# Overflow tables at the end of the expert stage, and the first two experts' transposes behind other products

## The chip, the cores and the metric

The program runs on one core of a Trainium2 chip. The metric is the device time of one execution in microseconds (us). The kernel before was run three times.

## The reference, cut to what matters

One encoder layer over 1024 tokens of width 1024: a combined projection, differential attention and an S5 state-space mixer side by side, an output projection with a first LayerNorm, and a hierarchical mixture of experts (4 groups of 8, two experts for each token) with a second LayerNorm. The change lies in the mixture of experts:

```python
def block_fn(args):                       # one block of 128 rows of one expert
    tok, w, e = args
    xb = h2d[tok]
    hid = jax.nn.silu(xb @ w_gate[e]) * (xb @ w_up[e])
    yb = hid @ w_down[e]
    return yb * w[:, None].astype(yb.dtype)
...
out = jnp.zeros_like(h2d).at[row_tok].add(ys.reshape(n_rows, -1).astype(h2d.dtype))
...
x = _layernorm(alpha * h + moe, ln2_g[i], ln2_b[i])
```

There are 32 experts. Each has a gate and an up matrix of 1024x512 and a down matrix of 512x1024, all in float32 (6 MB for each expert).

## The kernel before, in words

The early stages (projections, state-space mixer, attention, output projection, router) end at about 555 us of the profiled execution. The expert stage then runs to about 1152 us, and a closing stage adds up the two results of each token, normalizes and stores.

**One expert** takes up to 128 tokens. GpSimd gathers their rows (`gather`, L1136) into a slot of `gx`. `tokens(e)` (L1196) transposes the rows on TensorE, eight 128x128 transposes into the PSUM tile `xT`, and `split` (L172) turns that into a high part (a cast on ScalarE) and a low part (a subtraction on VectorE) in `xe`; a product of float32 numbers is made from three products of such parts. `product(e, m)` runs the matrix products, 12 for each half matrix: (e, g0), (e, u0), (e, g1), (e, u1), and later (e, d0), (e, d1). `gate` (silu on ScalarE) and `gated` (a product on VectorE) make the hidden rows, `turn_hidden` transposes them (four transposes into `hT`) and splits them into `he`, and `result` scales and adds on ScalarE and VectorE, scatters the rows to `moe_dram` (L1141) and gathers the rows of expert e+5.

**The weights** come in 192 half matrices of 1 MB, in the order of the list `order`: the gate and up halves of expert e, then the down halves of expert e-1. SyncE loads each (`load_next`) into a ring of 12 slots (15 at the start), so half matrix n is loaded once number n-12 has been split. `split_next` splits each into a ring of three pairs of slots: behind product n stands the split of half matrix n+3, and it waits until product n has read its pair. The loop at L1344 writes these steps in one order, and `keep_order` pins that order on all five engines from the first gather on. An instruction therefore waits behind everything that stands before it on its engine.

**The overflow tables.** An expert with more than 128 tokens needs further blocks. `overflow_blocks` (L1256) counts the tokens of each expert (one product `counts` on TensorE, L1265), makes `meta` (how many further blocks, and of which expert), and then `place` and `blk` (which token stands where), in 25 small VectorE instructions over a borrowed ring slot, the area `over`. Before the change `load_next` calls it where half matrix 63 is loaded, in the middle of the expert stage, about at expert 7.

**After the last expert** SyncE loads the second LayerNorm's gain and offset into the tile `lnc` (L1368 and L1369, 512 KB each, one row copied to all partitions). Each engine reads the number of further blocks from `meta` (L1375), and a loop over them follows (L1376). With these inputs it runs no turn, but its entry and exit are a meeting point: SyncE waits there until every engine has arrived and every transfer has landed. Behind it SyncE loads the rows of `moe_dram` into `mo` (L1444, L1446), GpSimd adds others on the way (L1452), VectorE takes the moments, and the normalized rows go out.

The PSUM banks of the gate and up products are two in all (`bank`, L131): g and u of expert 1 take over the banks of g and u of expert 0, and so wait until `gate(0)` and `gated(0)` have read them.

Of the kernel before, what the change touches and what calls it, by code (L numbers as in the profile page):

```python
# [19 lines left out]
P = 128  # L20
# [3 lines left out]
KT = D // P  # L24
NH = 4
NG = 32
NE = 32
# [87 lines left out]
def tile_kernel(ctx: ExitStack, tc: tile.TileContext, I: dict, out: bass.AP, dbg=None):  # L115
# [9 lines left out]
    sl = Slots()  # L125
# [982 lines left out]

    w_g, w_u, w_d = I["w_exp_gate"][0], I["w_exp_up"][0], I["w_exp_down"][0]
    NRAW, NSPL, NXG = 12, 3, 5  # L1110
    NOVER = 63

    NLENT = 3
    raw_ring = early + sl.take(NRAW + NLENT - len(early))
# [29 lines left out]
    order = []  # L1144
# [14 lines left out]

    def load_next():  # L1160
        n = st_["load"]
        if n == NOVER:
            over.extend(overflow_blocks(deep(n)[0]))
        e, m = order[n]
        j = int(m[1])
        slot = deep(n)[0]
        if m[0] == "d":
            r = sl.at(slot, [P, 2, D], F32, f"rw{e}{m}")
            src = w_d[e, 256 * j:256 * j + 256, :].rearrange("(p k) n -> p k n", p=P)
            for ks in (slice(0, 1), slice(1, 2)) if n == len(order) - 1 else (slice(0, 2),):  # L1170
                SP.dma_start(r[:, ks, :], src[:, ks, :])
        else:
            r = sl.at(slot, [P, 4, 512], F32, f"rw{e}{m}")
            src = w_g if m[0] == "g" else w_u
            SP.dma_start(r, src[e, 512 * j:512 * j + 512, :].rearrange("(p k) n -> p k n", p=P))
        raws[e, m] = r
        st_["load"] += 1
# [15 lines left out]
        hls[e, m] = (a, b)  # L1193
        st_["split"] += 1

    def tokens(e):  # L1196

        g_ = gx(e)
        b_ = bank2(f"xT{e}")
        for kt in range(KT):  # L1200
            PE.transpose(b_[:, kt * P:(kt + 1) * P], rows(g_, kt), ident)  # L1201
        xT[e] = t_ = xes[e % 2]
        split(t_[:, 0], t_[:, 1], b_.rearrange("p (k q) -> p k q", k=KT))

    def gate(e):
        S.activation(hd[:, 0, :], acc.pop((e, "g")), AF.Silu)
# [44 lines left out]
            gather(gx(e + NXG), idx[:, 0, e + NXG:e + NXG + 1])  # L1251


    over = []

    def overflow_blocks(key):  # L1256
        op = Area(sl, 1, "over", key)

        def rtile(name, shape):
            return op.get(f"{name}{shape}", shape)  # L1260

        m128 = rtile("m128", [7])
        ts(m128, iof[:, 1:8], float(P), ALU.mult)
        pr = bank("counts", 1)[:, 0:NE]
        PE.matmul(pr, one, Sx[:, NT, :], start=True, stop=True)  # L1265
        ovc = rtile("wide", [NE, 7])
        V.tensor_tensor(out=ovc, in0=bc(pr, 2, [NE, 7]), in1=bc(m128, 1, [NE, 7]), op=ALU.is_gt)
        ovn = rtile("ovn", [NE])
        V.tensor_reduce(out=ovn, in_=ovc, axis=AX.X, op=ALU.add)
        onef = rtile("onef", [NE])  # L1270
        V.memset(onef, 1.0)
        ove = rtile("ove", [NE])
        V.tensor_tensor_scan(out=ove, data0=onef, data1=ovn, initial=0.0, op0=ALU.mult, op1=ALU.add)
        ovs = rtile("ovs", [NE])
        sub(ovs, ove, ovn)
        metaf = rtile("metaf", [1 + MAXOV])
        V.tensor_copy(metaf[:, 0:1], ove[:, NE - 1:NE])
        for j in range(0, MAXOV, 5):
            ocmp = rtile("wide", [5, NE])
            V.tensor_tensor(out=ocmp, in0=bc(ove, 1, [5, NE]), in1=bc(iof[:, j:j + 5], 2, [5, NE]), op=ALU.is_le)  # L1280
            V.tensor_reduce(out=metaf[:, 1 + j:6 + j], in_=ocmp, axis=AX.X, op=ALU.add)
        ts(metaf[:, 1:1 + MAXOV], metaf[:, 1:1 + MAXOV], float(NE - 1), ALU.min)
        meta = cp.tile([P, 1 + MAXOV], I32, name="meta")
        V.tensor_copy(meta, metaf)
        ob = rtile("ob", [2, NT])
        for k in range(2):
            to = rtile("wide", [NT, NE])
            mul(to, bc(ovs, 1, [NT, NE]), O[:, k])
            V.tensor_reduce(out=ob[:, k], in_=to, axis=AX.X, op=ALU.add)
        q7 = rtile("q7", [2 * NT, 7])  # L1290
        V.tensor_tensor(out=q7, in0=bc(rk.rearrange("p k t -> p (k t)"), 2, [2 * NT, 7]),
                        in1=bc(m128, 1, [2 * NT, 7]), op=ALU.is_ge)
        qd_ = rtile("qd_", [2, NT])
        V.tensor_reduce(out=qd_.rearrange("p k t -> p (k t)"), in_=q7, axis=AX.X, op=ALU.add)
        place = cp.tile([P, 2, NT], F32, name="place")
        stt(place, qd_, -float(P), rk, ALU.mult, ALU.add)

        blk = cp.tile([P, 2, NT], F32, name="blk")
        add(blk, ob, qd_)
        stt(blk, qd_, 1.0, blk, ALU.min, ALU.mult)  # L1300
        ts(blk, blk, 1.0, ALU.subtract)
        op.close()
        return meta, place, blk

    def keep_order():

# [32 lines left out]
    with tc.issue_after(routed.ins), tc.issue_after(turned.ins):  # L1339
        split_next()  # L1340
        split_next()
        tokens(0)
        split_next()
    for n, (e, m) in enumerate(order):  # L1344
        refill()
# [6 lines left out]
            gated(e)  # L1352
        if m == "d1":
            result(e)
        if m == "u1" and e == 0:
            turn_hidden(0)
        if st_["split"] < len(order):
            split_next()
        if m == "u1" and e + 1 < NE:
            tokens(e + 1)  # L1360
        if m == "d0" and e + 1 < NE:
            turn_hidden(e + 1)
    keep_order()
    meta, place, blk = over
    sl.back([deep(n)[0] for n in range(len(order) - NRAW, len(order))])

    lnc = sl.get([P, 2, D], F32, "lnc")
# [148 lines left out]
```

## Time and profile before

| what | value |
|---|---|
| median of 3 runs | 1210.49 us (1209.18 to 1210.93) |
| the profiled execution | 1210.23 us, its span 1208.3 us |
| TensorE busy, share of the span | 1085.0 us, 90% |
| VectorE busy | 971.7 us, 80% |
| ScalarE busy | 704.4 us, 58% |
| GpSimd busy | 357.2 us, 30% |
| read from and written to HBM | 254.12 MB and 27.26 MB |
| granted TensorE clock, mean | 0.939 of full speed |

Engine names in rows: PE is TensorE's matrix products, PEld its weight loads, DVE is VectorE, ACT is ScalarE, POOL is GpSimd, SP is SyncE; a name with q is that engine's queue of instructions. Times are microseconds from the start of the span. `out<-in` gives what an instruction writes and reads, and brackets give how long its engine had been idle before it and what ended that.

### The profile page before, as it was taken

How to read it: one execution, taken by the hardware profiler on the slowest of the kernel's cores; microseconds unless marked ns; L12 is line 12 of the kernel's file. 1: busy time of each engine (PE TensorE's matmuls, PEld its weight loads, DVE VectorE, ACT ScalarE, POOL GpSimd, SP SyncE). 2: the span in 40 equal slices, each digit the busy share in tenths (PEclk: the TensorE clock that was granted, in tenths of full speed). 3: DMA queues.
4: the chain of work that ended last, by engine and by line, in shares of the span. 5: the costliest groups of instructions: out<-in, count | busy, mean ns of one | idle time of the engine just before them, and what ended most of it. 6: DMA issues, size and time to landing. Idle time of an engine off the chain costs nothing. (4 is left out here: it accounts for less than half of the span.)

```text
span 1208.3 us, 15031 instructions
## 1 busy us (share of the span) xinstructions
PE 1085.0 (90%) x5313; PEld 902.5 (75%) x5313; DVE 971.7 (80%) x1409; ACT 704.4 (58%) x941; POOL 357.2 (30%) x279
## 2 busy tenths in 40 slices
PE   7997998898899999995899998999999999999900
PEld 5876787776688788884688877888888888888800
DVE  4598578557877674456799999999999999999848
ACT  3222333445675643223588886888888888888702
POOL 0058455322344452342022121221122122121024
PEclk9998999998899999986899998999999999999955
DMA  5641111211101464454599998999999999999075
GB/s 198 157 89 48 43 40 45 58 36 36 55 16 36 140 214 140 191 207 175 196 358 387 375 369 313 374 385 392 379 379 380 379 375 386 393 377 389 29 258 175
DMA packets 89213, 271.01 MB, mean 224 GB/s; under 512 B 30128, under 2 KB 50608, under 8 KB 64688
## 3 DMA queue, kind: packets, MB, share of 16 engines
q1 hardware_dynamic: 65968, 245.18, 54.0%
q0 software_dynamic: 11216, 23.61, 6.8%
q10 hardware_dynamic: 11952, 1.23, 0.8%
q8 instruction: 43, 0.70, 0.2%
q14 instruction: 34, 0.28, 0.1%
HBM read 254.12 MB, written 27.26 MB: 233 GB/s over the span
## 5 line engine op out<-in xcount | busy, mean ns | idle before, releaser
L1141 POOL DMA_INDIRECT moe_dram<-yo,idx x32 | 54.0, 1688 | 461.9 <-DVE yo L164 456.6
L233 PE MATMUL proj<-xh,wb 128*128 128x512 f32 x256 | 76.2, 410 | 1.6 <-ACT ssm L674 1.6
L233 PE MATMUL proj<-xh,wa 128*128 128x512 f32 x256 | 76.0, 403 | 1.6 <-ACT ssm L674 1.6
L1071 PE MATMUL mix<-woh,mx 128*128 128x512 f32 x256 | 73.8, 399 | 0.7 <-DVE mx L155 0.7
L1136 POOL DMA_INDIRECT gx<-h_dram,idx x32 | 60.3, 1884 | 24.0 <-DVE WT L161 14.6
L786 ACT ACTIVATE p<-s,nm 128x1024 f32<-128x1024 f32 (+7 forms) x64 | 47.2, 742 | 25.3 <-DVE nm L799 19.6
L233 PEld LDWEIGHTS proj<-xh,wb 128*128 128x128 f32 x256 | 50.1, 199 | 12.2 <-ACT ssm L674 1.8
L233 PEld LDWEIGHTS proj<-xh,wa 128*128 128x128 f32 x256 | 48.5, 193 | 11.3 <-ACT ssm L674 1.8
L1071 PEld LDWEIGHTS mix<-woh,mx 128*128 128x128 f32 x256 | 47.6, 190 | 10.3 <-DVE mx L155 1.2
L1247 ACT ACTIVATE yo<-y,WT 128x1024 f32<-128x1024 f32 (+1 forms) x33 | 36.0, 1093 | 31.3 <-PE y L1231 31.3
L781 PE MATMUL s<-kk,qh 128*128 128x512 f32 (+3 forms) x96 | 41.1, 428 | 11.2 <-ACT p L786 10.3
L164 DVE SCALAR_TENSOR_TENSOR yo<-gx,first,yo 128x1024 f32<-128x1024 f32 (+1 forms) x33 | 41.2, 1252 | 6.3 <-ACT yo L1247 5.6
L799 DVE TENSOR_REDUCE nm<-s 128x1 f32<-128x1024 f32 (+3 forms) x32 | 32.6, 1020 | 13.1 <-PE s L783 13.1
L233 PE MATMUL proj<-xl,wa 128*128 128x512 f32 x128 | 42.8, 404 | 0.0
L233 PE MATMUL proj<-xl,wb 128*128 128x512 f32 x128 | 42.6, 408 | 0.0
L1201 PEld LDWEIGHTS xT<-ident,gx 128*128 128x128 f32 x256 | 36.5, 207 | 8.1 <-DMA gx<-h_dram,idx 6.0
L1201 PE MATMUL xT<-ident,gx 128*128 128x128 f32 x256 | 37.1, 290 | 5.7 <-DMA gx<-h_dram,idx 5.7
L155 DVE TENSOR_TENSOR xe<-xT,xe 128x1024 fp32r<-128x1024 f32 x32 | 39.0, 1218 | 3.9 <-ACT xe L174 3.9
L1071 PE MATMUL mix<-wol,mx 128*128 128x512 f32 x128 | 42.0, 397 | 0.0
L819 PE MATMUL po<-vv,half 128*128 128x128 f32 x288 | 41.3, 283 | 0.2 <-ACT half L816 0.2
L174 ACT CAST xe<-xT 128x1024 fp32r<-128x1024 f32 x32 | 32.1, 1004 | 12.6 <-PE xT L1201 12.6
L174 ACT CAST wb<-misc 128x512 fp32r<-128x512 f32 x16 | 9.7, 622 | 47.9 <-DMA misc<-in_w_in_dram 38.3
(862 smaller groups left out, 3560.8 us busy)
## 6 DMA issues: line engine op xcount, KB each, us to landing
misc<-in_w_in_dram SPq DMA_DIRECT2D x16, 512.0 KB, 4.1
mo<-moe_dram SPq DMA_DIRECT2D x11, 512.0 KB, 8.7
xr<-in_x_dram SPq DMA_DIRECT2D x8, 512.0 KB, 6.5
wo_raw<-in_w_out_dram SPq DMA_DIRECT2D x4, 1024.0 KB, 4.8
xa<-in_x_dram SPq DMA_DIRECT2D x8, 512.0 KB, 4.7
h_dram<-xa SPq DMA_DIRECT2D x8, 512.0 KB, 4.8
out_dram<-mo SPq DMA_DIRECT2D x8, 512.0 KB, 3.0
mo<-moe_dram POOLq DMA_DIRECT2D x5, 512.0 KB, 12.3
```

What stands on the lines that cost most here:

```text
L155: eng.tensor_tensor(out=out_, in0=a, in1=b, op=ALU.subtract)
L164: return V.scalar_tensor_tensor(out=out_, in0=a, scalar=s, in1=b, op0=op0, op1=op1)
L174: S.copy(hi, raw)
L233: PE.matmul(o[:, hs], wt[kt // 4][:, w_, kt % 4, :], x_[:, hs], start=(kt == 0 and n == 0), stop=(kt == KT - 1 and n == 2))
L781: PE.matmul(s_[:, c0:c0 + w], qd[0][:, c, tk], kk[h][:, c, c0:c0 + w], start=True, stop=False)
L786: S.activation(p_[:, c, 0:n], s_[:, 0:n], AF.Exp, bias=nm[:, c:c + 1], accum_out=L[:, j, c:c + 1])
L819: PE.matmul(po[:, j * P:(j + 1) * P], aT[:, k, :], vv[k // 4][:, k % 4, h * P:(h + 1) * P], start=(k == 0), stop=(k == i))
L1071: PE.matmul(o[-(hs.start > 0)][:, hs], mx[:, m_, kt, :], (woh, wol)[w_][kt // 2][:, kt % 2, hs], start=(kt == 0 and n == 0), stop=(kt == K ...
L1136: return G.indirect_dma_start(out=dst, out_offset=None, in_=h_dram[:, :], in_offset=bass.IndirectOffsetOnAxis(ap=ix, axis=0), bounds_check ...
L1141: G.indirect_dma_start(out=moe_dram[:, :], out_offset=bass.IndirectOffsetOnAxis(ap=ix, axis=0), in_=src, in_offset=None, bounds_check=2 * ...
L1201: PE.transpose(b_[:, kt * P:(kt + 1) * P], rows(g_, kt), ident)
L1247: S.mul(yo[:, hs], y[:, hs], WT[:, e:e + 1])
```

## The change

There are three edits.

1. `overflow_blocks` is cut in two. The first part, up to `meta`, is called behind product (30, d1) and `result(30)`. The second, `overflow_places`, which makes `place` and `blk`, is called behind the whole loop. Both work in the area `over`, now in the ring slot of half matrix 180 (expert 30, g1). The call in `load_next` is gone.
2. `tokens` takes a number of parts. Expert 0's transposes come in two halves, each with its own split; all other experts' in one.
3. `tokens(1)` stands behind product (0, u0) and no longer behind (0, u1). `turn_hidden(0)` stands behind product (1, u0) and no longer behind (0, u1).

```diff
@@ load_next
-        if n == NOVER:
-            over.extend(overflow_blocks(deep(n)[0]))
@@ tokens
-    def tokens(e):
+    def tokens(e, parts=1):
 
         g_ = gx(e)
         b_ = bank2(f"xT{e}")
-        for kt in range(KT):
-            PE.transpose(b_[:, kt * P:(kt + 1) * P], rows(g_, kt), ident)
         xT[e] = t_ = xes[e % 2]
-        split(t_[:, 0], t_[:, 1], b_.rearrange("p (k q) -> p k q", k=KT))
+        n = KT // parts
+        for k0 in range(0, KT, n):
+            for kt in range(k0, k0 + n):
+                PE.transpose(b_[:, kt * P:(kt + 1) * P], rows(g_, kt), ident)
+            split(t_[:, 0, k0:k0 + n], t_[:, 1, k0:k0 + n], b_[:, k0 * P:(k0 + n) * P].rearrange("p (k q) -> p k q", q=P))
@@ overflow_blocks
         V.tensor_copy(meta, metaf)
+        return meta, m128, ovs
+
+    def overflow_places(m128, ovs):
...
-        op.close()
-        return meta, place, blk
+        return place, blk
@@ the start of the stage and its loop
-        tokens(0)
+        tokens(0, 2)
         split_next()
...
-        if m == "u1" and e == 0:
-            turn_hidden(0)
         if st_["split"] < len(order):
             split_next()
-        if m == "u1" and e + 1 < NE:
+        if (e, m) == (0, "u0") or m == "u1" and 0 < e < NE - 1:
             tokens(e + 1)
+        if (e, m) == (1, "u0"):
+            turn_hidden(0)
         if m == "d0" and e + 1 < NE:
             turn_hidden(e + 1)
+        if (e, m) == (NE - 2, "d1"):
+            meta, *parts = overflow_blocks(deep(len(order) - NRAW)[0])
+    place, blk = overflow_places(*parts)
     keep_order()
```

Three places in the engines' rows show it. First ScalarE at the start of the expert stage; `xe` is the split of a token tile, `wh` the high part of a weight half, `gx<-g` the silu, `he` the split of the hidden rows. Before:

```order
L174 CAST xe_4368<-xT_4424 128x1024
L174 CAST wh0g_4435<-rw0g_4377 128x1024 x2
L174 CAST wh0u_4460<-rw0u_4379 128x1024 x2
L174 CAST wh1g_4479<-rw1g_4381 128x1024 x2
L1206 ACT_TABLE_LOAD
L1206 ACTIVATE gx_4367<-g_4447 128x512
L174 CAST wh1u_4498<-rw1u_4383 128x1024 x2
L174 CAST he<-hT_4528 128x512
L174 CAST wh1g_4535<-rw1g_4385 128x1024 x2
L174 CAST xe_4369<-xT_4541 128x1024
```

Now:

```order
L174 CAST xe_4368<-xT_4424 128x512 x2
L174 CAST wh0g_4437<-rw0g_4377 128x1024 x2
L174 CAST wh0u_4462<-rw0u_4379 128x1024 x2
L174 CAST wh1g_4481<-rw1g_4381 128x1024 x2
L174 CAST xe_4369<-xT_4487 128x1024
L1205 ACT_TABLE_LOAD
L1205 ACTIVATE gx_4367<-g_4449 128x512
L174 CAST wh1u_4511<-rw1u_4383 128x1024 x2
L174 CAST wh1g_4541<-rw1g_4385 128x1024 x2
L174 CAST wh1u_4562<-rw1u_4387 128x1024 x2
L174 CAST wh0d_4583<-rw0d_4389 128x1024 x2
L174 CAST he<-hT_4589 128x512
```

Expert 0's token tile is cast in two halves, expert 1's token tile has moved ahead of the first silu, and the hidden rows of expert 0 come later. On TensorE the eight transposes of expert 0 still stand in one row ahead of the first product.

Second, VectorE at the end of the expert stage, in the new order, from the last instruction of the first part on:

```order
L1283 CAST meta<-over 128x16
L164 SCALAR_TENSOR_TENSOR yo<-gx_4366,first,yo 128x512 x2
L158 TENSOR_TENSOR over<-over,LR 128x256
L1294 TENSOR_REDUCE over<-over 128x8
L158 TENSOR_TENSOR over<-over,LR 128x256
L1294 TENSOR_REDUCE over<-over 128x8
L1296 TENSOR_TENSOR over<-rk,over 128x112
L1299 TENSOR_REDUCE over<-over 128x16
L164 SCALAR_TENSOR_TENSOR place<-over,rk 128x16
L161 TENSOR_TENSOR blk<-over 128x16
L164 SCALAR_TENSOR_TENSOR blk<-over,blk 128x16
L168 TENSOR_SCALAR blk<-blk 128x16
```

`yo` is the scaled result of expert 31. The 15 instructions up to `meta` now stand between the results of expert 30 and of expert 31, which were neighbours before, and the other ten behind the last result.

Third, SyncE's queue at the same place, with the semaphores that each row waits for (DMAHW are its own transfers, DMASW those of GpSimd). Before:

```order
L1171 DMA rw31d_8931<-in_w_exp_down_dram 128x1024 [waits DMAHW0_49]
L1368 DMA lnc<-in_ln_g_dram 128x1024 [waits DMAHW1_49,DVE_49]
L1369 DMA lnc<-in_ln_b_dram 128x1024 [waits DMAHW2_49]
L1376 COMPARE_AND_BRANCH
L1376 UNCONDITIONAL_BRANCH [waits SP_sequencer_49,DMAHW0_49,DMAHW3_49,DMAHW4_49,DMAHW5_49,DMAHW6_49,DMAHW7_49]
```

Now:

```order
L1168 DMA rw31d_8902<-in_w_exp_down_dram 128x1024 [waits DMAHW0_49]
L1381 TENSOR_LOAD meta [waits DVE_49]
L1381 ISA x2
L1374 DMA lnc<-in_ln_g_dram 128x1024 [waits DMAHW1_49,DVE_49,Activation_49]
L1382 COMPARE_AND_BRANCH
L1382 UNCONDITIONAL_BRANCH [waits SP_sequencer_49,DMAHW2_49,DMAHW3_49,DMAHW4_49,DMAHW5_49,DMAHW6_49,DMAHW7_49]
```

Behind the loop the queue goes on like this:

```order
L1375 DMA lnc<-in_ln_b_dram 128x1024
L1450 DMA mo_9405<-moe_dram 128x1024
L1452 DMA mo_9405<-moe_dram 128x1024
```

The read of `meta`, which stood in the middle of SyncE's row, now stands ahead of the load of the gain, and the load of the offset has moved behind the loop, directly ahead of the first load of `mo`. The exit of the loop waits for all eight of SyncE's transfer semaphores, before and now.

## Rows read from the trace of the kernel before

**Rows 1.** Windows (busy by engine: PE, PEld, DVE, ACT, POOL; clock, DMA share, GB/s).
```profile
720.00:760.00 40.00, 34.95 (x153) 28.79 (x153) 38.02 (x55) 26.83 (x29) 7.41 (x4) 0.91 0.84 322
760.00:800.00 40.00, 40.00 (x192) 33.71 (x191) 38.52 (x37) 33.47 (x37) 7.42 (x4) 1.00 0.98 377
```

**Rows 2.** Timeline of PE (start, length, instruction), 718 to 765 us.
```profile
719.46 1.11 PE L1201 MATMUL xT<-ident,gx 128*128 128x128 f32 x8
...
728.40 1.13 PE L1214 MATMUL hT<-ident,gx 128*128 128x128 f32 x4 [5.05 <-DVE gx L158]
...
744.89 1.11 PE L1201 MATMUL xT<-ident,gx 128*128 128x128 f32 x8
...
762.73 1.11 PE L1201 MATMUL xT<-ident,gx 128*128 128x128 f32 x8
```

**Rows 3.** Timeline of DVE, 718 to 765 us: the overflow tables.
```profile
720.75 0.17 DVE L168 TENSOR_SCALAR over<-iof 128x7 f32<-128x7 f32 x1
...
724.76 0.42 DVE L158 TENSOR_TENSOR over<-over,LR 128x256 f32<-128x256 f32 x1
...
727.37 0.17 DVE L164 SCALAR_TENSOR_TENSOR blk<-over,blk 128x16 f32<-128x16 f32 x1
```

**Rows 4.** Timeline of PE, 545 to 612 us: the start of the expert stage.
```profile
556.35 1.99 PE L1201 MATMUL xT<-ident,gx 128*128 128x128 f32 x8 [5.75 <-DMA gx<-h_dram,idx]
559.49 0.79 PE L1240 MATMUL g<-wh0g,xe 128*128 128x512 f32 x1 [1.15 <-ACT xe L174]
...
564.08 0.40 PE L1240 MATMUL u<-wh0u,xe 128*128 128x512 f32 x1
...
569.54 0.39 PE L1240 MATMUL u<-wh0u,xe 128*128 128x512 f32 x1
...
575.65 0.74 PE L1214 MATMUL hT<-ident,gx 128*128 128x128 f32 x4 [3.23 <-DVE gx L158]
...
579.87 0.79 PE L1240 MATMUL g<-wh1g,xe 128*128 128x512 f32 x1 [1.88 <-ACT xe L174]
...
601.44 0.39 PE L1240 MATMUL g<-wh2g,xe 128*128 128x512 f32 x1
```

**Rows 5.** Windows, columns as in rows 1.
```profile
580.00:584.00 4.00, 3.55 (x8) 2.34 (x9) 1.49 (x2) 0.00 (x0) 0.00 (x0) 0.50 0.67 215
```

**Rows 6.** Timelines of ACT and of DVE, 545 to 612 us.
```profile
569.78 1.28 ACT L1206 ACT_TABLE_LOAD   x1 [0.75 <-issue]
...
576.43 0.58 ACT L174 CAST he<-hT 128x512 fp32r<-128x512 f32 x1 [2.89 <-PE hT L1214]
...
574.91 0.68 DVE L158 TENSOR_TENSOR gx<-u,gx 128x512 f32<-128x512 f32 x1
```

**Rows 7.** Timelines of DVE and of PE, 1100 to 1209 us.
```profile
1150.56 1.41 DVE L164 SCALAR_TENSOR_TENSOR yo<-gx,first,yo 128x512 f32<-128x512 f32 x2 [4.84 <-ACT yo L1247]
...
1144.48 0.74 PE L1231 MATMUL y<-wh31d,he 128*128 128x512 f32 x2 [0.77 <-DVE he L155]
```

**Rows 8.** The chain that ended last (start, length, what), and SyncE's waits, from 1100 us.
```profile
1152.25 3.18 DMA moe_dram<-yo,idx
...
1169.37 9.26 DMA mo<-moe_dram
...
SPq L1368 <- DVE wl30g L155: 3.3, 1, 3.3
```

**Rows 9.** Landing of the first LayerNorm's gain and offset (tile lnb); page's DMA issues.
```profile
DMA to landing us min/median/max: 4.1/4.5/4.9
...
out_dram<-mo SPq DMA_DIRECT2D x8, 512.0 KB, 3.0
```

**Rows 10.** Groups of the page, and timeline of POOL, 1100 to 1209 us: the scatters.
```profile
L1141 POOL DMA_INDIRECT moe_dram<-yo,idx x32 | 54.0, 1688 | 461.9 <-DVE yo L164 456.6
...
1152.25 0.97 POOL L1141 DMA_INDIRECT moe_dram<-yo,idx  x1 [5.28 <-DVEq L1376]
```

**Rows 11.** DMA issues of 1000 to 1100 us: count, KB each, us to landing.
```profile
rw31g<-in_w_exp_gate_dram SPq DMA_DIRECT2D x2, 1024.0 KB, 8.0
```

More of the change, by code (lines that the diff above doesn't have):

```diff
@@ L1110, in tile_kernel @@
     NRAW, NSPL, NXG = 12, 3, 5
-    NOVER = 63
     NLENT = 3
@@ L1251, in result @@
             gather(gx(e + NXG), idx[:, 0, e + NXG:e + NXG + 1])
-    over = []
+    over = {}
     def overflow_blocks(key):
-        op = Area(sl, 1, "over", key)
+        op = over["area"] = Area(sl, 1, "over", key)
         def rtile(name, shape):
@@ L1284, in overflow_blocks, with rtile @@
         V.tensor_copy(meta, metaf)
+        return meta, m128, ovs
+    def overflow_places(m128, ovs):
+        def rtile(name, shape):
+            return over["area"].get(f"{name}{shape}", shape)
         ob = rtile("ob", [2, NT])
@@ L1354, in tile_kernel @@
             result(e)
-        if m == "u1" and e == 0:
-            turn_hidden(0)
         if st_["split"] < len(order):
             split_next()
-        if m == "u1" and e + 1 < NE:
+        if (e, m) == (0, "u0") or m == "u1" and 0 < e < NE - 1:
             tokens(e + 1)
+        if (e, m) == (1, "u0"):
+            turn_hidden(0)
         if m == "d0" and e + 1 < NE:
             turn_hidden(e + 1)
+        if (e, m) == (NE - 2, "d1"):
+            meta, *parts = overflow_blocks(deep(len(order) - NRAW)[0])
+    place, blk = overflow_places(*parts)
     keep_order()
-    meta, place, blk = over
     sl.back([deep(n)[0] for n in range(len(order) - NRAW, len(order))])
```

## The prediction, made before the changed kernel was run

> **What bounds the kernel now.** I read the windows first, to see which engine is full in which stretch; then TensorE's timeline, to see where the full stretches break; then the timelines of the engines it waited for; and last the chain that ended last, for what follows the experts. From 760 to 800 us, a stretch of plain expert work, TensorE is busy 40.0 of 40 us at full clock, VectorE 38.5, and the DMA share is 0.98 [rows 1]. The reader should see one full engine and two nearly full ones. TensorE sets the pace: the token transposes of two neighbouring experts start at 744.89 and 762.73, so a period is 17.84 us, with no idle time named in its rows [rows 2].
>
> That pace breaks at two places in the stage. In the stretch 720 to 760 TensorE is busy only 34.95 us and the clock is 0.91 [rows 1]: the hidden-row transposes at 728.40 came after 5.05 us of idle, released by a VectorE product [rows 2] that stood behind the overflow tables, which fill VectorE from 720.75 to 727.5 [rows 3]. And at the start TensorE waits 3.23 us for the hidden rows of expert 0 and 1.88 us for the tokens of expert 1 [rows 4], and works at half clock (0.50) behind these pauses [rows 5]. Behind the experts nothing but latency counts: the last scatter lands at 1152.25 + 3.18 = 1155.43, only then do the loads of `mo` start, and transfers lead the chain from there [rows 8].
>
> **Edit 1a, tables out of the middle.** The period that holds them lasted 744.89 - 719.46 = 25.43 us; 25.43 - 17.84 = 7.59 us go [rows 2]. That is the 5.05 us of idle and the half clock behind it. What is late next? VectorE's own period, which has 1.5 us to spare in 40 [rows 1], as in all other periods; so I take the whole 7.6. SyncE's read of `meta` leaves the middle too; the loads behind it were early anyway.
>
> **Edit 1b, part one at the end.** From its first instruction to the start of part two it took 724.76 - 720.75 = 4.0 us [rows 3]. It now stands between the last two `yo`, where VectorE was idle 4.84 us, waiting for ScalarE [rows 7]. Cost: nothing, with 0.8 us to spare; with the cover gone the last scatter would come later by what exceeds it. The count product stands ahead of (31, d0), in which TensorE waits 0.77 us for VectorE [rows 7], so it is hidden too; a whole 512-column product, far larger, lasts 0.40 [rows 4].
>
> **Edit 1c, part two and what queues behind it.** It lasts 727.37 + 0.17 - 724.76 = 2.78 us [rows 3]. It starts when the last `yo` ends, 1150.56 + 1.41 = 1151.97 [rows 7], so the last reader of the area `over` ends at 1154.75. By itself that is hidden, because the scatter lands at 1155.43. But the gain load waits for it: in the run before SyncE waited at L1368 for `wl30g` [rows 8], that is for the ring slot of expert 30's g1, and this very slot now holds `over`. The load, issued before in the shade of the last weights, is now issued at 1154.75. The loop's exit waits for its landing, and so does everything behind. Its duration here is not in the trace. From below: a 512 KB store to HBM with the queues idle, 3.0 us; the nearest row is the same kind of load, the first LayerNorm's gain and offset, 4.1 us for the faster of the two [rows 9]; from above, 8.0 us for a 1 MB weight load under full traffic [rows 11]. I take 4.1, since it is the same shape with little beside it: 1154.75 + 4.1 = 1158.85, which is 3.4 us behind the scatter. The Trainium skill, page "DMA: Bandwidth & Descriptors", section "Anatomy of one DMA — SWDGE (gpsimd) path", gives about 2.0 us fixed plus the bytes over 436 GB/s, which for 512 KB makes an estimate of 3.2 us; by it the sum would be 0.9 us lower.
>
> The offset load has moved behind the loop, ahead of the first `mo` load. The transfers there lead the chain (9.26 us of one piece of it [rows 8]), so its 0.524 MB at the 377 GB/s of [rows 1] are 1.4 us more; from below 0.3 us if only the issue counts. Together the end costs 3.4 + 1.4 = **4.8 us**, between 2.6 (3.0 landing, 0.3) and 8.7 (8.0 landing, 1.4).
>
> **Edit 2, expert 0 in halves.** TensorE's order still has all eight transposes ahead of the first product, and the second half's PSUM tile is the one that the first half's split reads. If the second four wait for that split: four transposes (half of 1.99 [rows 4]) 1.0, half a cast 0.58 and half a subtraction 0.68 [rows 6], four transposes 1.0, and some 0.2 of handing over make 3.5 us from 556.35, so the first product starts at 559.8 instead of 559.49 [rows 4]. In return its third part no longer waits for the low half. I cost it at **nothing**, between 0.6 us lost and 0.6 us gained.
>
> **Edit 3, transposes behind other products.** From 564.08, the start of (0, u0), to 601.44, the start of (2, g0), TensorE took 37.36 us [rows 4]. In it stand nine products, two token transposes and two hidden-row transposes. Six products and one of each transposes make a period; so at full pace this is 1.5 periods, 26.76, and half of one pair of transposes, some 0.7 (1.11 [rows 2] and 0.74 [rows 4], overlapping): 27.5 us. So 9.9 us are lost there now. With `tokens(1)` behind (0, u0) its split has two products of time; with `turn_hidden(0)` behind (1, u0), `gated(0)` has two. Expert 1's rows were gathered directly behind expert 0's, which had landed at 556.35, so I cost their earlier use at nothing; late rows would show as a wait of `xT`.
>
> What is late next is (1, u0): it takes over the bank of (0, u0) and waits for `gated(0)`. That chain is not changed: table load at 569.78 (0.24 behind the start of (0, u1) at 569.54 [rows 4]), silu, one weight split and the product, to 575.65: 5.87 us [rows 4, 6]. TensorE has two products, (0, u1) and (1, g0), to fill 0.24 + 5.87 = 6.1 us; a product is about (17.84 - 1.3) / 6 = 2.76 us, so it waits 6.1 - 5.5 = 0.6 us. That is no pause in which the clock is likely to fall. Gain: 9.9 - 0.6 = **9.3 us**, between 8.0 (a wait of 1.9 us, as the token wait before) and 9.9.
>
> **The sum.** -7.6 + 4.8 + 0 - 9.3 = -12.1 us. The sum stands against the profiled execution, 1210.23 us (span 1208.3), which is 0.3 us below the median of the three runs: **1198.1 us**. With the bounds of its terms this case lies mostly between 1195 and 1202.
>
> **The rivals.**
> *The end is cheaper:* the exit does not wait for the gain's landing, or the landing hides beside the scatter. Then only the offset's 1.4 us stay: 1210.2 - 9.3 - 7.6 + 1.4 = 1194.7. For it: the scatter itself ends the wait before [rows 8]. Against it: the new row of the exit names all eight transfer semaphores, and the load starts 0.7 us ahead of the scatter's end. In this case part two's second neighbour counts: scatters issued beside a busy VectorE last 1.69 us on average, the last one, with VectorE idle, 0.97 [rows 10]; part two would run beside it, so some 0.7 us would be added. The Trainium skill, page "SBUF — State Buffer", section "Who interferes with whom", goes further: GpSimd and VectorE share a port pair, held exclusively, so an instruction of VectorE that takes it blocks GpSimd's writing of descriptors. By that, at the most the whole 2.78 us, this rival would give 1197.5; the two rows agree with the rule in sign, at a quarter of that size.
>
> *The front keeps its half clock:* of the 9.9 us, 3.23 + 1.88 = 5.1 are idle [rows 4] and 4.8 are half clock and small waits. If the new wait at (1, u0), or late weight splits behind the first silu, make a pause after which TensorE works at 0.50 again [rows 5], those 4.8 stay: 1198.1 + 4.8 = 1202.9. For it: VectorE has about one split for each product, without much room. Against it: a pause of 0.6 us stands against the 3.23 us behind which the clock was seen at 0.50.
>
> *Slower, the weights set the pace:* the DMA share is 0.98 [rows 1]; if the ring can't be filled faster than it is, ScalarE's casts at the head of the splits wait for weights, what was gained at front and middle is waited for later, and only the end's cost stays: 1210.2 + 4.8 = 1215.0. It decides from the point at which a load lands later than the ring is deep: it is issued 12 splits ahead, two periods, 35.7 us. Against it: the last experts' loads still land 8.0 us after issue [rows 11], after some twenty periods at the unbroken pace.
>
> That edit 2 does not do what it says is in the forecast already.
>
> **How the numbers follow.** Forecast 0.78, cheaper end 0.07, half clock kept 0.10, weights 0.03, something else that eats it all 0.02. The range takes the forecast's own spread from 1195 to 1202, the cheaper end, and the nearer half of the clock's case: 1194.5 to 1202.5; left out are the weights and the far ends. A measurement of this kernel tells 0.2% (2.4 us) from no change; the first three cases are all faster by more: 0.95, within 0.2% 0.02, slower 0.03.
>
> **What would show it.** Right: no idle of several us ahead of any `hT` in TensorE's timeline, (2, g0) about 9 to 10 us earlier, 17.84 us between all later token transposes, a short wait of (1, u0) for `gx` of VectorE; part one between the last two `yo`; SyncE's gain load issued about 2.8 us behind the last `yo`, and the loop's exit released by its landing, 3 to 4 us behind the scatter. Wrong: an exit released by the scatter (cheaper end), a clock of 0.50 between 565 and 590 us (clock kept), or ScalarE's casts waiting for `rw` (weights).

## The result and the profile after

The changed kernel took **1198.0 us** (median of four runs, 1195.34 to 1199.21), the kernel before on the same chip 1210.71 (four runs, 1209.18 to 1213.46). The ratio is 0.9888, with a 95% interval of 0.9871 to 0.9906. Forecast were 1198.1 us, 1194.5 to 1202.5, and faster. The profiled execution took 1199.21 us, its span 1197.5, where before had 1210.23 and 1208.3.

The reader should not compare whole spans first, but stages. The program ahead of the first token transposes (the first `xT`) is the same in all kernels here (e5 and e11 add one small ScalarE instruction), yet in the thirteen profiled executions these start anywhere between 556.24 and 562.44 us. So I cut every span at four starts that TensorE's and VectorE's timelines name: the first `xT`, the `xT` of expert 2, that of expert 31, and the last `yo` on VectorE. From the `xT` of expert 31 to the last `yo` it is 31.2 us in every kernel; that column is left out. The stages of a row are those of one execution.

| kernel | first xT at | front: to xT of expert 2 | middle: to xT of expert 31 | end: last yo to end of span | runs' median, us | ratio (95%) |
|---|---|---|---|---|---|---|
| before | 556.35 | 38.14 | 524.84 | 57.74 | 1210.71 | 1 |
| after | 559.26 | 29.44 | 517.06 | 60.52 | 1198.0 | 0.9888 (0.9871 to 0.9906) |
| e1_tables_only | 558.31 | 39.07 | 517.07 | 60.65 | 1208.28 | 0.9978 (0.9966 to 0.999) |
| e2_front_only | 561.00 | 29.61 | 524.58 | 56.57 | 1205.11 | 0.9943 (0.9921 to 0.9965) |
| e3_whole0 | 558.65 | 29.34 | 517.08 | 60.83 | 1199.37 | 0.991 (0.9892 to 0.9928) |
| e4_over_elsewhere | 560.93 | 29.39 | 517.06 | 56.51 | 1196.19 | 0.987 (0.9845 to 0.9895) |
| e5_table_early | 557.15 | 28.36 | 517.06 | 56.41 | 1195.41 | 0.9886 (0.9863 to 0.9909) |
| e6_tok_moved | 557.84 | 33.56 | 517.08 | 60.92 | 1202.13 | 0.9931 (0.991 to 0.9952) |
| e7_hid_moved | 561.02 | 36.11 | 517.06 | 60.39 | 1205.49 | 0.9956 (0.994 to 0.9973) |
| e8_offset_behind | 562.44 | 29.55 | 517.08 | 64.82 | 1203.57 | 0.994 (0.9919 to 0.9962) |
| e9_middle_in_two | 556.24 | 30.05 | 523.42 | 56.43 | 1203.71 | 0.994 (0.9917 to 0.9963) |
| e10_offset_early | 558.71 | 29.03 | 517.07 | 58.99 | 1197.0 | 0.989 (0.9871 to 0.991) |
| e11_own_banks | 557.31 | 25.82 | 517.06 | 56.50 | 1192.86 | 0.9844 (0.9825 to 0.9864) |

From before to after the columns differ by +2.9, -8.7, -7.8 and +2.8 us, together the -10.8 us of the two spans. The first of these is not the change's.

Stages of the same code differ between executions too, and the reader should keep that beside every difference below. The front of e1 is that of before and took 39.07 us for 38.14: between 6 and 8 us behind the first transposes the granted clock was 0.50 in e1 and 0.89 in before. The seven fronts that hold edit 3 whole and neither e5's nor e11's edit go from 29.03 to 30.05 us, and the ends of before, e2 and e9, which have the same code there, from 56.43 to 57.74. So a difference of about 1 us between two single rows is not shown by them alone.

**The middle.** The two windows of [rows 1], in the changed kernel:

```profile
720.00:760.00 40.00, 40.00 (x189) 33.50 (x188) 38.97 (x38) 33.25 (x36) 8.37 (x5) 1.00 0.99 393
760.00:800.00 40.00, 40.00 (x189) 33.52 (x188) 39.00 (x36) 32.80 (x36) 10.16 (x6) 1.00 1.00 384
```

Both stretches are full at full clock now; the 34.95 us and the clock of 0.91 of [rows 1] are gone.

**The front.** Timeline of TensorE, 556 to 600 us, against [rows 4], and the windows there (columns as in rows 1) against [rows 5]:

```profile
559.26 1.13 PE L1201 MATMUL xT<-ident,gx 128*128 128x128 f32 x4 [5.75 <-DMA gx<-h_dram,idx]
561.84 1.13 PE L1201 MATMUL xT<-ident,gx 128*128 128x128 f32 x4 [1.45 <-DVE xe L155]
562.62 0.77 PE L1239 MATMUL g<-wh0g,xe 128*128 128x512 f32 x1
...
567.25 0.39 PE L1239 MATMUL u<-wh0u,xe 128*128 128x512 f32 x1
...
569.98 1.11 PE L1201 MATMUL xT<-ident,gx 128*128 128x128 f32 x8
...
579.90 0.47 PE L1239 MATMUL u<-wh1u,xe 128*128 128x512 f32 x1 [0.61 <-DVE gx L158]
...
595.64 0.39 PE L1239 MATMUL g<-wh2g,xe 128*128 128x512 f32 x1
```
```profile
560.00:564.00 4.00, 2.55 (x9) 1.92 (x8) 1.06 (x2) 1.58 (x3) 0.00 (x0) 0.50 0.91 318
564.00:568.00 4.00, 4.00 (x14) 3.17 (x13) 2.68 (x3) 2.03 (x3) 0.00 (x0) 0.69 0.17 53
568.00:572.00 4.00, 4.00 (x23) 3.47 (x22) 3.11 (x3) 3.28 (x4) 0.00 (x0) 1.00 0.64 246
...
580.00:584.00 4.00, 4.00 (x20) 3.36 (x21) 4.00 (x4) 2.55 (x4) 0.00 (x0) 1.00 0.31 68
```

The waits of 3.23 and 1.88 us are gone, one wait of 0.61 us at (1, u0) has come, and the clock, once at 1.00, stays there. Two things the reader should also see: expert 0's second four transposes wait 1.45 us for the split of the first half, and the clock is at 0.50 until behind that pause.

**The end.** VectorE's timeline shows both parts of the tables around the last `yo`; SyncE's shows when the loads behind them are issued:

```profile
1130.88 1.28 DVE L164 SCALAR_TENSOR_TENSOR yo<-gx,first,yo 128x1024 f32<-128x1024 f32 x1
1132.08 0.16 DVE L168 TENSOR_SCALAR over<-iof 128x7 f32<-128x7 f32 x1
...
1136.00 0.17 DVE L1283 CAST meta<-over 128x16 int32<-128x16 f32 x1
1136.98 1.42 DVE L164 SCALAR_TENSOR_TENSOR yo<-gx,first,yo 128x512 f32<-128x512 f32 x2 [0.81 <-ACT yo L1246]
1138.31 0.42 DVE L158 TENSOR_TENSOR over<-over,LR 128x256 f32<-128x256 f32 x1
...
1140.91 0.18 DVE L164 SCALAR_TENSOR_TENSOR blk<-over,blk 128x16 f32<-128x16 f32 x1
```
```profile
1141.16 0.34 SPq L1374 DMA_DIRECT2D lnc<-in_ln_g_dram  x1
1145.45 0.33 SPq L1375 DMA_DIRECT2D lnc<-in_ln_b_dram  x1
1145.83 0.43 SPq L1450 DMA_DIRECT2D mo<-moe_dram  x1
```

Part one fits, with 0.81 us of idle left in front of the last `yo`, where it had 4.84 [rows 7]. SyncE's waits from 1100 us, and the chain that ended last, tell what the loop's exit (L1382) waited for:

```profile
SPq L1374 <- DVE blk L164: 4.1, 1, 4.1
...
SPq L1382 <- DMA lnc<-in_ln_g_dram: 2.1, 1, 2.1
```
```profile
1141.16 3.63 DMA lnc<-in_ln_g_dram
1149.04 10.22 DMA mo<-moe_dram
```

The gain's landing has taken the scatter's place in the chain [rows 8]. And GpSimd's issue of the last scatter, beside part two on VectorE, takes as long as the one with VectorE idle [rows 10]:

```profile
1138.68 0.97 POOL L1140 DMA_INDIRECT moe_dram<-yo,idx  x1 [5.26 <-DVE yo L164]
```

### The profile page after: what moved, and what is told of

It is laid out like the page before. It is cut to its first block, busy times and chain, and to the rows that moved or that the text cites. A ratio compares the mean times of both kernels' runs of the same rounds, so it can differ in the third digit from the quotient of the medians.

```text
span 1197.5 us, 15035 instructions
## 1 busy us (share of the span) xinstructions
PE 1078.5 (90%) x5313; PEld 898.3 (75%) x5313; DVE 972.9 (81%) x1410; ACT 704.2 (59%) x942; POOL 358.3 (30%) x279
## 4 chain that ended last, share of the span: by engine, by line
PE 62%; DVE 5%; DMA 2%; issue 1%; ACT 1%; SPq 0%; DVEq 0%; POOL 0%; ACTq 0%; POOLq 0%
PE g L1239 14%; PE y L1230 14%; PE u L1239 14%; PE mix L1071 7%; PE xT L1201 3%; PE po L819 2%; PE glu L729 2%; DMA mo<-moe_dram 2%; PE hT L1213 1%; PE pl L1093 1%; PE s L781 1%; PE at L815 1%; PE s L782 1%; DVE mo L161 1%; PE hT L1089 1%
## 5 line engine op out<-in xcount | busy, mean ns | idle before, releaser
L233 PEld LDWEIGHTS proj<-xh,wb 128*128 128x128 f32 x256 | 49.5, 196 | 12.1 <-ACT ssm L674 1.8
L155 DVE TENSOR_TENSOR xe<-xT,xe 128x1024 fp32r<-128x1024 f32 (+1 forms) x33 | 39.1, 1186 | 4.4 <-ACT xe L174 4.4
L174 ACT CAST xe<-xT 128x1024 fp32r<-128x1024 f32 (+1 forms) x33 | 32.3, 978 | 13.7 <-PE xT L1201 13.7
L819 PEld LDWEIGHTS po<-vv,half 128*128 128x128 f32 x288 | 36.6, 195 | 1.8 <-ACT half L816 0.4
```

What stands on the lines that cost most here:

```text
L155: eng.tensor_tensor(out=out_, in0=a, in1=b, op=ALU.subtract)
L233: PE.matmul(o[:, hs], wt[kt // 4][:, w_, kt % 4, :], x_[:, hs], start=(kt == 0 and n == 0), stop=(kt == KT - 1 and n == 2))
L819: PE.matmul(po[:, j * P:(j + 1) * P], aT[:, k, :], vv[k // 4][:, k % 4, h * P:(h + 1) * P], start=(k == 0), stop=(k == i))
```

## The experiments

The medians carry the scatter of the unchanged first 556 us and more (runs of before went from 1206.07 to 1214.45), so where a microsecond decides I go by the stages of the table.

**One edit at a time.** e1_tables_only takes back edits 2 and 3:

```
-        tokens(0, 2)
+        tokens(0)
...
+        if m == "u1" and e == 0:
+            turn_hidden(0)
...
-        if (e, m) == (0, "u0") or m == "u1" and 0 < e < NE - 1:
+        if m == "u1" and e + 1 < NE:
             tokens(e + 1)
-        if (e, m) == (1, "u0"):
-            turn_hidden(0)
```


> Edit 1 alone: tables at the end in two parts, the first experts in the order of the kernel before. Theory A (the terms of the prediction add up): -7.6 in the middle and +4.8 at the end, -2.8 us, about 1207.9 against 1210.7. Theory B (the end is cheaper, as the changed kernel's trace suggests: from the start of the last yo to the end of the span 60.52 us instead of 57.74, +2.8): -4.8 us, about 1205.9. Rival C (the stall in the middle was not the tables' doing, so the 7.6 us come back elsewhere): slower than before by the end's cost, 1213.5 to 1215.5. TensorE's timeline should show no idle of 5 us ahead of any hT from expert 2 on, and 3.2 us of idle ahead of the hT of expert 0 as before.

e2_front_only is the reverse: the kernel before with these lines the other way round, and its tables where they were.

> Edits 2 and 3 alone: the tables stay in the middle, where they were. Theory A (the prediction): -9.3 us, about 1201.4. Theory B (the changed kernel's trace: expert 2's transposes stand 29.44 us behind expert 0's instead of 38.14): -8.7 us, about 1202.0. Rival C (part of the front's gain needs the tables out of the way, or is given back at the stall in the middle, where the ring of weights would be fuller or emptier): less than 6 us, above 1204.7. The idle of about 5 us ahead of one hT in the middle should stand as before.

Measured: e1's median is 2.3 us below before's of the same rounds (1210.56), e2's 5.5, and after's was 12.7 below. That looks as if the two halves did not add up. By stages they do, within the scatter: e1's middle is 517.07, as in after, and its end 60.65; e2's front is 29.61, its middle 524.58, its end 56.57. From the first `xT` to the end of the span before took 651.95 us, e1 647.99, e2 642.00, after 638.24: -3.96 and -9.95 make -13.91, and after has -13.71 (that it fits to 0.2 us is luck, since e1's front alone lost 0.9). The medians miss 5.0 us; in the profiled executions 3.7 lie ahead of the first `xT`, which starts later than before's by 1.96 us in e1 and 4.65 in e2, but by 2.91 in after. By its median e2 would be rival C's (less than 6 us); by its stages rival C falls, since nothing is given back in the middle, and e1's rival C too. The -3.96 of e1 lie between its theories A and B. In the timelines of TensorE, e1 has the old waits of the front and e2 the old one of the middle:

```profile
579.11 1.13 PE L1213 MATMUL hT<-ident,gx 128*128 128x128 f32 x4 [3.23 <-DVE gx L158]
...
583.72 0.79 PE L1239 MATMUL g<-wh1g,xe 128*128 128x512 f32 x1 [1.77 <-ACT xe L174]
```
```profile
724.50 1.13 PE L1216 MATMUL hT<-ident,gx 128*128 128x128 f32 x4 [5.05 <-DVE gx L158]
```

One more thing came out: e2's end code is that of before, and it took 56.57 us against 57.74. The end itself varies by 1.2 us between executions.

**The tables' lump, cut in two but left in the middle.** e9_middle_in_two is e2 with part two one expert later, in a ring slot of its own (what both parts use stands outside the ring slots):

```
         if n == NOVER:
-            over.extend(overflow_blocks(deep(n)[0]))
+            over["one"] = overflow_blocks(deep(n)[0])
+        if n == NOVER + 6:
+            over["two"] = overflow_places(*over["one"][1:], deep(n)[0])
...
```


> Edits 2 and 3 with the tables left in the middle, but in their two parts, one expert apart (4.0 and 2.78 us of VectorE). Theory A (VectorE runs ahead by a slack of 6.8 - 5.05 = 1.7 us, and only what exceeds it stalls TensorE): idle of 2.3 us ahead of one hT and of 1.0 us ahead of the next, the two periods together 3.3 us over 35.66 instead of 7.4 over; about 1201, 4 us faster than e2. Rival B (every pause of 2 us and more also halves the clock, as the ones of 3.23 and 5.05 us did): 5 to 6 us over, 1203.5. Rival C (the slack is gone at once and every microsecond of tables is a microsecond of stall): 6.8 us over, 1204.5.

TensorE's timeline of e9:

```profile
711.47 1.12 PE L1206 MATMUL xT<-ident,gx 128*128 128x128 f32 x8
...
717.38 0.74 PE L1218 MATMUL hT<-ident,gx 128*128 128x128 f32 x4 [2.03 <-DVE gx L158]
...
733.20 1.12 PE L1206 MATMUL xT<-ident,gx 128*128 128x128 f32 x8
...
738.28 0.75 PE L1218 MATMUL hT<-ident,gx 128*128 128x128 f32 x4 [1.19 <-DVE gx L158]
```

The idle times, 2.03 and 1.19 us, are those of theory A (2.3 and 1.0): only what exceeds VectorE's lead stalls TensorE. The time is that of rival B: the periods that begin at the `xT` before each pause last 21.73 and 19.31 us, 5.4 over the two plain ones. Behind the 2.03 us the granted clock is 0.80 and 0.78 in two windows of 4 us; behind the 1.19 it stays at 1.00. So cutting the lump saves 2 of its 7.6 us (less by the table's column, since all periods of this profile last 17.86 us); taking it out of the middle saves all.

**Edit 2 alone.** e3_whole0 changes one line, `tokens(0, 2)` to `tokens(0)`.

> The changed kernel without edit 2: expert 0's eight transposes and its split in one piece again. Theory A (edit 2 is worth nothing, between 0.6 us lost and 0.6 us gained): 1198.0, within 1197.4 to 1198.6. Rival B (the halves hurt: the second four transposes wait 1.45 us for the first half's split, and the clock rises later behind that pause, at 564 to 568 us instead of 562 to 564): 1 to 1.5 us faster than the changed kernel, about 1196.7. Rival C (the halves help: the third part of each product's columns comes earlier): 1 us slower, about 1199.

The front takes 29.34 us against 29.44, and from the first `xT` to the end of the span it is 638.4 against 638.2: theory A. The median, 1199.37 against 1198.0, would be rival C's, but the intervals overlap and the stages show nothing of it. Halves gain nothing here; e11 below shows why.

**The two halves of edit 3.** e6_tok_moved moves only expert 1's token transposes, e7_hid_moved only expert 0's hidden-row transposes.

> The changed kernel with half of edit 3: expert 1's token transposes behind (0, u0), but expert 0's hidden-row transposes behind (0, u1), where they stood before. Theory A (each pause costs itself and the clock behind it): the wait of 3.23 us for the hidden rows stays with half a clock behind it, only the token wait of 1.88 us and the small waits go; from the first token transposes to those of expert 2 some 34 to 36 us (before 38.14, changed 29.44), so 1203 or so. Rival B (the clock fell because of the token wait): about 32.5 us, since only the 3.23 us stay. Rival C (the token transposes were the whole gain): 30 us or less.

> The changed kernel with the other half of edit 3: expert 0's hidden-row transposes behind (1, u0), but expert 1's token transposes behind (0, u1), where they stood before. Theory A (each pause costs itself and, from 2 to 3 us on, some 1.5 to 2.7 us of half clock behind it): the token wait of 1.88 us stays with little or no half clock, the hidden-row pause of 3.23 us goes; from the first token transposes to those of expert 2 about 31.5 us (changed 29.44, tokens moved alone 33.56, before 38.14). Rival B (the token wait alone brings the clock down as far as both did): 34 us or more. Rival C (the hidden rows were the whole gain): below 30 us.

e6's front is 33.56 us, 4.6 less than before; e7's 36.11, 2.0 less; both together gain 8.7. e6 lies between theory A (34 to 36) and rival B (32.5). The wait of 3.23 us stays, and the granted clock is 0.82 in the 4 us around its end (576 to 580) and 0.75 in the next four, with no token wait there: so the mechanism is theory A's, its size a little smaller. e7 is a miss of theory A: its time is rival B's, but not by rival B's reason alone. TensorE's timelines of e6 and of e7:

```profile
578.34 1.05 PE L1213 MATMUL hT<-ident,gx 128*128 128x128 f32 x4 [3.23 <-DVE gx L158]
```
```profile
581.24 0.50 PE L1239 MATMUL g<-wh1g,xe 128*128 128x512 f32 x1 [3.02 <-ACT xe L174]
583.89 1.22 PE L1239 MATMUL g<-wh1g,xe 128*128 128x512 f32 x2 [1.78 <-DVE xe L155]
```

In e7 the token wait, for the high and then for the low parts, is 3.02 + 1.78 = 4.80 us. In before it is 1.88 [rows 4] and, for the low parts, 0.45 (TensorE's timeline of before):

```profile
581.54 1.22 PE L1240 MATMUL g<-wh1g,xe 128*128 128x512 f32 x2 [0.45 <-DVE xe L155]
```

ScalarE's timeline of e7 tells why it grew: the cast of expert 1's tokens stands behind silu and two casts of weights.

```profile
575.91 0.60 ACT L1205 ACTIVATE gx<-g 128x512 f32<-128x512 f32 x1
576.41 1.99 ACT L174 CAST wh1u<-rw1u 128x1024 fp32r<-128x1024 f32 x2
578.29 1.99 ACT L174 CAST wh1g<-rw1g 128x1024 fp32r<-128x1024 f32 x2
580.18 1.01 ACT L174 CAST xe<-xT 128x1024 fp32r<-128x1024 f32 x1
```

The transposes start at 577.11, but the cast not before 580.18. While TensorE stood for the hidden rows, this work went by unseen; with that pause gone, TensorE reaches (1, g0) earlier and waits there. Of 3.23 us taken away, 4.80 - 2.33 = 2.47 came back. The rest of the 2.0 us goes with the clock: the granted clock is 0.79 in the 16 us from 576 in e7, and 0.68 in the 16 us from 574 in before. Hence the two moves are worth more together than one by one (8.7 against 4.6 + 2.0): with the tokens moved as well, their cast stands ahead of silu.

**The new wait at (1, u0).** e5_table_early is e4 (next) with one small Silu ahead of expert 0's casts:

```
         split_next()
         split_next()
+        S.activation(hd[:, 0, 0:8], WT[:, 0:8], AF.Silu)
         tokens(0, 2)
```


> The kernel with the tables' area in another ring slot (e4), and one 8-column Silu on ScalarE ahead of expert 0's casts, where ScalarE waits for the gathered rows anyway, so that the table of functions (1.28 us) is loaded there and not ahead of the silu of expert 0. Theory A (the wait of 0.6 us at (1, u0) hangs on that table load): that wait is gone, the first three token transposes span 28.8 us instead of 29.4, and the run is 0.6 us faster than e4, about 1195.6. Rival B (the wait hangs on VectorE, which is late with the weight splits in front of gated(0)): the wait stays within 0.1 us of 0.6, 1196.2. Rival C (the casts bring another table in again, so the load stays): no change.

ScalarE's timeline of e5: the table now loads while ScalarE waits, and silu of expert 0 waits for its product alone, where after has the load in front of it (first fence after, second e5).

```profile
573.93 1.28 ACT L1205 ACT_TABLE_LOAD   x1 [0.85 <-issue]
```
```profile
551.63 1.28 ACT L1346 ACT_TABLE_LOAD   x1 [5.22 <-DVE WT L161]
552.92 0.21 ACT L1346 ACTIVATE gx<-WT 128x8 f32<-128x8 f32 x1
...
571.93 0.60 ACT L1205 ACTIVATE gx<-g 128x512 f32<-128x512 f32 x1 [1.15 <-PE g L1239]
```

The wait of 0.6 us at (1, u0) is not in its timeline any more, and the front takes 28.36 us against e4's 29.39: theory A, and 0.4 us more than it asked for. This is beyond the scatter: from the `xT` of expert 1 to that of expert 2 it is 17.84 us in e5, the plain period, and 18.68 to 18.74 in all seven kernels with edit 3 whole and the table load in its old place. The medians (1195.41, 1196.19) cannot tell this apart.

**The end.** e4_over_elsewhere puts the tables' area into another ring slot; e10_offset_early leaves it, but gives the offset a slot of its own; e8_offset_behind leaves it, and issues the offset behind the loads of `mo`:

```
-            meta, *parts = overflow_blocks(deep(len(order) - NRAW)[0])
+            meta, *parts = overflow_blocks(deep(len(order) - 2)[0])
```
```
-    lnc = sl.get([P, 2, D], F32, "lnc")
-    SP.dma_start(lnc[:, 0, :], I["ln2_g"][0].partition_broadcast(P))
-    SP.dma_start(lnc[:, 1, :], I["ln2_b"][0].partition_broadcast(P))
+    lnc = [sl.get([P, 2, D], F32, f"ln{k}") for k in range(2)]
+    SP.dma_start(lnc[0][:, 0, :], I["ln2_g"][0].partition_broadcast(P))
+    SP.dma_start(lnc[1][:, 0, :], I["ln2_b"][0].partition_broadcast(P))
...
```
```
-    SP.dma_start(lnc[:, 1, :], I["ln2_b"][0].partition_broadcast(P))
...
         mos.append(mo)
+    SP.dma_start(lnc[:, 1, :], I["ln2_b"][0].partition_broadcast(P))
```


> The changed kernel with the area of the tables in the ring slot of the second-last weight instead of the slot that the second LayerNorm's gain and offset take next. Nothing else moves but that both of those loads are issued ahead of the read of meta, as before the change. Theory A (the prediction's term 1c): the loop's exit no longer waits for the gain's landing, and no offset load stands ahead of the mo loads: 4.8 us faster than the changed kernel, about 1193.2. Theory B (its trace: +2.8 us net, because the tail takes up a part): about 1195.2. Rival C (the end's cost is part two itself, beside the last scatter, and not the load that waits): no change, 1198.0.

> The changed kernel with the second LayerNorm's offset in a ring slot of its own: its load is issued among the last weights, as before the change; the gain load still waits for the tables' end, and the loop's exit for the gain. From the start of the last yo to the first mo load the changed kernel took 8.85 us, with the area in another slot 5.67; to the end of the span 60.5 and 56.5. Theory A (the gain's landing costs 2.8 to 2.9 us, the offset's issue and traffic the other 1.1): first mo load at 8.5, end 59.4. Rival B (the offset's traffic was hidden): end 60.1 to 60.5. Rival C (the exit did not wait for the gain but for the offset ahead of the mo loads): first mo load at 5.7, end 56.5.

> The changed kernel with the offset load issued behind the loads of mo and not ahead of them; the gain load still waits for the tables' end. Theory A (the offset's 0.524 MB at the traffic's rate stand in the way): the end, from the start of the last yo to the end of the span, takes 1.4 us less than the changed kernel's 60.5, 59.1. Theory B (only its issue of 0.38 us counts): 60.1. Rival C (the whole end cost is the offset, not the gain that the loop's exit waits for): 56.5, as with the area in another slot.

The end takes 56.51 us in e4, 58.99 in e10, 60.52 in after, 64.82 in e8. The chain of e4, then SyncE's timelines of e4 and of e10:

```profile
1140.28 3.19 DMA moe_dram<-yo,idx
1147.36 8.71 DMA mo<-moe_dram
```
```profile
1144.26 0.34 SPq L1450 DMA_DIRECT2D mo<-moe_dram  x1
```
```profile
1140.14 0.34 SPq L1374 DMA_DIRECT2D ln<-in_ln_g_dram  x1
1144.29 0.33 SPq L1450 DMA_DIRECT2D mo<-moe_dram  x1
```

In e4 the scatter ends the wait again, with part two still beside it, so its rival C falls: part two costs nothing by itself, and the end, 56.51 us, is that of e2 and e9 (56.57, 56.43), which have the code of before there. e4's last `yo` starts at 1138.59, e10's at 1136.01, after's at 1136.98, so the first load of `mo` is issued 5.67, 8.28 and 8.85 us behind it. The gain's landing therefore costs 8.28 - 5.67 = 2.6 us at the first load and 58.99 - 56.51 = 2.5 at the end; the offset ahead of `mo` costs 60.52 - 58.99 = 1.5: theory A of e10, and of e4 with 4.0 us for the 4.8 expected.

e8 is a plain miss: no theory had it slower. SyncE's and VectorE's timelines show the reason:

```profile
1156.66 0.33 SPq L1453 DMA_DIRECT2D lnc<-in_ln_b_dram  x1
...
1170.12 2.74 DVE L164 SCALAR_TENSOR_TENSOR mo<-mo,rstd,lnc 128x512 f32<-128x512 f32 x4 [4.08 <-DMA lnc<-in_ln_b_dram]
```

Issued at 1156.66 behind eleven loads, the offset landed 13.4 us later, and the normalization stood still for it. So e8 says nothing on the 1.5 us, which is why e10 was made.

**Why the halves gained nothing, and the fastest version.** e11_own_banks is e5 with a PSUM tile for each half of expert 0's transposes:

```
-        b_ = bank2(f"xT{e}")
...
         for k0 in range(0, KT, n):
+            b_ = bank2(f"xT{e}_{k0}")
```


> The fastest kernel so far (e5: tables' area in another slot, table of functions loaded early), with each half of expert 0's transposed rows in a PSUM tile of its own. Theory A (edit 2 gained nothing because the second four transposes wait 1.45 us for the split of the first half, whose tile they share): the second four follow the first without that wait, the first product starts some 2.1 us behind the first transposes instead of 3.4, and the first three token transposes span 1 us or more less than e5's 28.36, about 27.2; 1194.3 against e5's 1195.4. Rival B (the halves gain nothing anyway, because the weights' splits or the half clock set the pace behind them): 28.3 within 0.3. Rival C (two pairs of banks for expert 0 delay expert 1's transposes): 28.8 or more.

TensorE's timeline, and the window behind it in e5 and in e11:

```profile
557.31 1.98 PE L1201 MATMUL xT<-ident,gx 128*128 128x128 f32 x8 [6.34 <-DMA gx<-h_dram,idx]
559.16 0.79 PE L1239 MATMUL g<-wh0g,xe 128*128 128x512 f32 x1
...
565.29 1.11 PE L1201 MATMUL xT<-ident,gx 128*128 128x128 f32 x8
...
583.13 1.11 PE L1201 MATMUL xT<-ident,gx 128*128 128x128 f32 x8
```
```profile
560.00:564.00 4.00, 4.00 (x13) 3.27 (x13) 2.24 (x3) 2.48 (x3) 0.00 (x0) 0.51 0.38 141
```
```profile
560.00:564.00 4.00, 4.00 (x18) 3.34 (x18) 3.15 (x4) 3.05 (x4) 0.00 (x0) 0.95 0.36 139
```

All eight transposes follow each other, the first product starts 1.85 us behind them (after: 3.36, before: 3.14), and the clock is already at 0.95 in the window in which e5 had 0.51. The front falls to 25.82 us, 2.5 less than e5, more than twice what theory A expected: 1.5 by the earlier start; the rest goes with the earlier clock. e11 was profiled once, but this is beyond the scatter: between 4 and 6 us behind the first transposes its granted clock is 1.00, and 0.50 in each of the other twelve executions. So the shared tile had cancelled edit 2. With a median of 1192.86 us and a ratio of 0.9844 (0.9825 to 0.9864), e11 is faster than the kernel before and than the changed one, whose interval begins at 0.9871. Against e5 (0.9863 to 0.9909) the intervals just touch, so that step rests on the stages.

## Why the prediction was right

**Edit 1a, -7.6 us:** right; e1, with the tables moved alone, has the whole 7.8 us of the middle column (7.6 of the one period, 0.2 of its neighbour).

**Edit 1b, 0:** right, down to the spare: 0.8 us forecast, 0.81 in the row.

**Edit 1c, +4.8:** mis-sized, by 0.8; mechanism right. The wait of the exit for the gain measured 2.5 to 2.6, not 3.4, mostly because the landing took 3.63 and 3.55 us (after, e10) where I took 4.1 from the first LayerNorm's loads [rows 9]; besides, SyncE's next load follows the gain's landing after 0.60 us (e10), the scatter's after 0.79 (e4). The offset's place measured 1.5 for 1.4. The Trainium skill, page "DMA: Bandwidth & Descriptors", section "Anatomy of one DMA — SWDGE (gpsimd) path", had led to an estimate of 3.2 us for that landing; the two landings lie between it and the row I used. That section is on transfers that GpSimd issues; SyncE issued these. Between the profiles of before and after the end grew by 2.8 only, but 1.2 us of that difference is scatter of the end itself, which e2 shows.

**Edit 2, 0:** right by its bounds; the first product starts 0.2 us later behind the transposes, and e3 shows no difference. The reason given, the shared PSUM tile, is shown by e11.

**Edit 3, -9.3:** from (0, u0) to (2, g0) after takes 595.64 - 567.25 = 28.39 us, forecast 28.1; so 9.0 of the 9.3 came. The new wait of (1, u0), 0.6 forecast, is 0.61, and e5 shows that it hangs on the table load. What the working did not see is that the two moves need each other (e6, e7).

**The sum.** The stages that the change touches make -8.7 - 7.8 + 4.0 = -12.5 us, forecast -12.1; the medians differ by 12.7. The terms stand up one by one; that the time is met to 0.1 us is luck. The unchanged stages ahead of the first `xT` scatter by 6 us between executions, the profiled execution after is 1.2 us above its median, and 0.8 us too much cost at the end stand against 0.3 to 0.6 too much gain at the front.

**The rivals.** The cheaper end is out: the exit waits for the gain (2.1 us at L1382). The row that the prediction leaned on shows less than it says: it names six of SyncE's transfer semaphores, DMAHW2 to DMAHW7, and not all eight; the wait itself is what shows it. The sub-case is out too, since the last scatter takes 0.97 us with part two beside it. The Trainium skill, page "SBUF — State Buffer", section "Who interferes with whom", has GpSimd blocked while an instruction of VectorE holds the shared ports, and it says which instructions do: on trn2 `tensor_reduce` never, and `tensor_tensor` on the read side alone, which (the section marks this as inferred) is not the side that descriptors are written through. A `tensor_reduce` and a `tensor_tensor` of part two ran while that scatter was issued, so the section, read whole, does not ask for a delay, and the trace agrees: 0.97 us. The prediction's "at the most the whole 2.78 us" left this list out, and its 1.69 us [rows 10] is the mean of scatters beside other work of VectorE. The half clock is out: from 567 to 600 us the granted clock is 1.00, and no pause above 0.61 us is left behind the first product. That weights set the pace is out: the middle's DMA share is 0.99 to 1.00, and the period is still 17.84 us.

## What to carry to other kernels

A lump of small work on an engine that feeds the full one costs what exceeds its lead plus the clock behind the pause; moved to where the same engine waits anyway, it costs nothing, but look then at which buffer the lump lives in, because a transfer that takes that buffer next moves with it (4.0 us here, and one number in the code takes them back). Two waits behind each other hide each other: cost them together, and expect that removing one alone pays only part. Filling and reading a tile in halves paid here only when the halves were tiles of their own (e11 against e3).

## What the runs showed of the hardware that I had not expected

A pause of TensorE of 2.03 us was followed by a granted clock of 0.80 and 0.78 (e9), so part of the time at 1.2 GHz, while pauses of 0.61 (after) and 1.19 us (e9) were followed by 1.00 throughout. In e11, taking a 1.45 us pause out of the first transposes went with a clock of 0.95 in the window in which e5 had 0.51; of the 2.5 us that the front gained, the first product's earlier start is 1.5, and this the other 1.0.

A 512 KB load landed 3.6 us after issue with little beside it (after, e10) and 13.4 us after issue behind eleven others (e8).

The unchanged first stages took 556.24 to 562.44 us in thirteen executions. Why stays open. The mean granted clock ahead of the first `xT` is 0.95 in the earliest (e9) and 0.93 in the latest (e8), but it is 0.94 in both before and after, which lie 2.9 us apart; so the clock is a part at most.
